# A two-layer attention trunk: shorter scale, gate and combine sequences on VectorE, and one more buffer each for the split q and k and for the split exponentials

## The chip, the core and the metric

The kernel runs on one core of a Trainium2 chip. The metric is the time of one execution on the device, in microseconds (us). The engines of the core are named as in the profile: PE (TensorE, matmuls), PEld (its weight loads), DVE (VectorE), ACT (ScalarE), POOL (GpSimd) and SP (SyncE), whose queue issues every DMA of this kernel. PE, DVE, ACT, POOL and SP each work through their own instructions in the order in which these stand, and wait for one another by semaphores. Lines are written as L345, line 345 of the kernel before.

## The reference, cut to what matters

```python
def reference(x, ...):                       # x: 1 x 1024 x 1024, 16 heads of 64
    for i in range(2):                       # layer 0: FoX, layer 1: dilated windows
        h = rms_norm(x, norm_g[i])
        o, gate = mixer_i(h, ...)
        x = x + (o * jax.nn.silu(gate)) @ w_out
    return x

def fox_mixer(h, ...):                       # causal attention with a forget term
    q, k = rms_norm(q, q_g), rms_norm(k, k_g)
    c = jnp.cumsum(jax.nn.log_sigmoid(f_logit), axis=1)
    s = q @ k * scale + c_q - c_k            # masked, softmax, times v

def dsw_mixer(h, ...):                       # 3 groups: (window, dilation)
    q, k = rotary(rms_norm(q)), rotary(rms_norm(k))
    for g, (window, dilation) in enumerate(((128, 1), (512, 4), (2048, 16))):
        o_g, lse_g = dilated_window_attention(q[g], k[g], v[g], window, dilation)
    wts = jax.nn.softmax(jnp.stack(lses, axis=0), axis=0)
    o = jnp.einsum('gbsh,gbshd->bshd', wts, jnp.stack(outs, axis=0))
```

## The kernel before, in words

**Numbers.** A product of two float32 matrices is made of three float16 products: each side is scaled by a power of two and split into a high and a low half (xh and xl for the rows, the two planes of `w` for the weights), and high times high, high times low and low times high are summed in PSUM (`project`, L340). The scores and the products with v are made in the same way.

**Weights.** They come in blocks of 1024 x 384 (class `Weights`): `load` brings four pieces `raw`, `bound` measures each (DVE L281 the pieces 0 and 2, ACT L279 the pieces 1 and 3, then two small ACT steps L284 and L285), `scale` spreads the measure over the partitions with a small matmul (L252) and works out a power of two in a chain of one-column DVE instructions (L254, L255, L241 to L243, L293, and for a q-k-v block L295, L296, L297 and L300, the last of which keeps a running minimum `low`), and `split` makes the two halves (ACT L310 and DVE L311; one piece of four on POOL, L313 and L315). All of this is done for the next block while the present one is multiplied.

**Stages.** `gates(0)` multiplies out the gate columns of layer 0 and writes silu of them to memory (`gs_d`). Then come 8 pairs of heads of the FoX layer, the output projection of layer 0, `gates(1)`, and 24 blocks of the second layer: 8 pairs of heads of group 0 first, then for each pair of heads the block of group 2 and the block of group 1. The output projection of layer 1 ends it.

**One block of q, k, v.** It has 8 tiles of 128 rows, 24 matmuls each, into one of three PSUM buffers `pj`. Of each tile, DVE multiplies q and k by gains into `u` (L433), ACT squares them (`sq`, L438), and v is split by ACT and DVE (L443, L444); L444 is the last reader of `pj`. For every second tile `heads_pair` normalises two tiles at once: sums (L451, L453), an inverse root by Ln and Exp on ACT (L471 to L473) with a correction on DVE (L474, L475), in layer 1 the rotation on POOL (L465 to L468), the product (L477), and the split of the result into `hl` (ACT L479, POOL L480, DVE L481). A DMA transpose (L485) turns `hl` into `qk_t`, from which PE makes scores (L505). There is one buffer `hl` (`hb=1`).

**Softmax.** Scores are masked and their running extreme is found by one DVE instruction (L745 in the FoX layer, L970 in layer 1), exponentials are taken on ACT (L546, L971), split into `ph` (ACT L549, POOL L552; in layer 1 L975, L976), transposed by DMA into `ptt` (L553, L977) and multiplied with v (L560 to L562). In both layers there are two buffers `ph` and three `ptt`.

**Putting three groups together.** Groups 0 and 2 write unnormalised sums, the row sum and the row extreme to memory (`og_d`, L1083). For each pair of tiles of group 1, `load_cmb` loads the two others and the gate (L1037, L1041), `weigh` finds the common extreme `mm` (DVE L998), makes three weights (POOL L1000, ACT L1001) and weighs and adds groups 0 and 2 on POOL (L1003, L1004), and `combine` on DVE weighs the group's own sums (L1011), adds (L1012), divides (L1014, L1016) and multiplies by the gate (L1019).

**What sets the order.** The order of PE is written out: `Flow` counts slots, four to a tile, and each step of the attention is hung on a slot (`LSD` and `LPD` are the slots from a tile to its scores and from there to the product with v). The order of the other engines is made when the program is built, by a scheduler that goes by priorities and its own estimates.

Of the kernel before, what the change touches and what calls it, by code (L numbers as in the profile page):

```python
# [22 lines left out]
P = 128  # L23
# [29 lines left out]
def tile_cols(g, t):  # L53


    if g < 2:
        return slice(t * P, (t + 1) * P, 1)
    a = 2 * P * (t % 4) + t // 4
    return slice(a, a + 2 * 127 + 1, 2)

# [23 lines left out]
def trunk(ctx, tc, ins, out, cfg):  # L84
# [143 lines left out]
    isx = const.tile([P, 2], F32, name="isx")  # L228
    sy = const.tile([P, 2], F32, name="sy")
    low = const.tile([P, 2], F32, name="low")  # L230
    nc.vector.memset(low, 2.0 ** 60)
# [6 lines left out]
    def root_floor(q):  # L238
# [7 lines left out]
    def spread_sums(src, n, lo, hi):  # L246
# [8 lines left out]
        nc.vector.tensor_scalar(v1, v1, lo, hi, ALU.max, ALU.min)  # L255
        return v1

    under = {}
    turned = set()

    class Weights:
# [10 lines left out]
        def bound(self, i):  # L272
# [4 lines left out]
            if i % 2:  # L277
                jk = sb.tile([P, 2, self.n], F16, name="jk", tag="jk", bufs=1)
                nc.scalar.activation(jk, raw, AF.Square, accum_out=self.vm[:, i : i + 1])  # L279
            else:  # L280
                nc.vector.tensor_reduce(self.vm[:, i : i + 1], raw, AX.XY, ALU.max, apply_absolute_value=True)  # L281
            if i == KT // 2 - 1:
                v = [a.rearrange("p (a b) -> p a b", b=2) for a in (self.vm, self.vm2)]
                nc.scalar.activation(v[1][:, :, 0], v[0][:, :, 0], AF.Square)  # L284
                nc.scalar.copy(v[1][:, :, 1], v[0][:, :, 1])  # L285

        def scale(self):

            e = root_floor(spread_sums(self.vm2, KT // 2, 2.0 ** -40, 2.0 ** 60))
            f = self.f = sm.tile([P, 5], F32, name="ws_f", tag="ws_f")  # L290
            self.sw, t2, self.inv = (f[:, i : i + 1] for i in range(3))
            by, ly = sy if self.kind == "out" else sx, slice(self.layer, self.layer + 1)
            nc.vector.tensor_scalar(self.sw.bitcast(I32), e, -1.0, float(268 << 23), ALU.mult, ALU.add)  # L293
            if self.kind == "qkv":
                nc.vector.tensor_scalar(t2, self.sw, by[:, ly], 2.0, ALU.mult, ALU.max)  # L295
                nc.vector.tensor_scalar(self.sw, t2, 2.0 ** 30, isx[:, ly], ALU.min, ALU.mult)  # L296
                nc.vector.tensor_scalar(t2, t2, 2.0 ** 30, None, ALU.min)  # L297
                self.t2, self.eps = t2, f[:, 3:4]
# [4 lines left out]
            if self.kind != "qkv":  # L303
                nc.vector.reciprocal(self.inv, t2)
# [869 lines left out]
```

## Time and profile before

| | |
|---|---|
| median of 3 runs | 1825.76 us (1823.03 to 1827.61) |
| the profiled execution | 1813.33 us, span 1811.5 us |
| granted PE clock over the span | 0.970 of full speed |
| busy share of the span | PE 92%, DVE 70%, ACT 59%, POOL 48% |
| DMA | 69.8% of 16 engines, 290.44 MB in one queue |

The profile is of one execution; the span runs from its first to its last instruction. A row of a group gives the count, the summed time and the mean of one instruction in ns; behind the bar stands the idle time of the engine just before them, and what ended it. A row of waits gives the total in us, how often, and the longest. A row of the timeline gives start, duration, engine, line and names; the bracket is the idle time before it and its releaser.

### The profile page before, as it was taken

The numbers are of one execution on the slowest core, as the hardware profiler recorded it, in microseconds if no ns is written. First come the engines' busy times: TensorE is split into PE (matmuls) and PEld (weight loads), VectorE is DVE, ScalarE is ACT, GpSimd is POOL, SyncE is SP. The second block draws the span as 40 slices with busy tenths as digits, with TensorE's granted clock in tenths as the row PEclk, the third lists the DMA queues.
The fourth block names the chain that finished last, engine by engine and source line by source line (L and its number), as shares of the span: only waits on it lengthen the run. The fifth ranks groups of instructions, "written<-read, shape, count | busy, mean of one in ns | idle before, by whom it ended". The sixth has DMA issues, their size and how long they took to land.

```text
span 1811.5 us, 38107 instructions
## 1 busy us (share of the span) xinstructions
PE 1659.2 (92%) x13342; PEld 1060.2 (59%) x13342; DVE 1259.9 (70%) x3906; ACT 1068.3 (59%) x2790; POOL 872.5 (48%) x1019
## 2 busy tenths in 40 slices
PE   5899898898888997999999989999899998999999
PEld 3566566566665433756666656656556565565654
DVE  8866677766776557766677786677776777767752
ACT  6555666666666546555666666556555565655630
POOL 4203555555554323125565545556475665646520
PEclk8999999999999998999999999999999999999999
DMA  7334998988889777336777787678676777767742
GB/s 260 122 138 103 191 192 174 168 171 195 191 174 209 205 218 225 109 108 139 141 151 168 149 185 152 138 150 164 153 154 141 157 154 158 161 140 153 190 125 91
DMA packets 658769, 292.88 MB, mean 162 GB/s; under 512 B 510208, under 2 KB 622848, under 8 KB 658576
## 3 DMA queue, kind: packets, MB, share of 16 engines
q1 hardware_dynamic: 658576, 290.44, 69.8%
q8 instruction: 104, 1.70, 0.4%
q14 instruction: 89, 0.73, 0.1%
HBM read 124.35 MB, written 41.22 MB: 91 GB/s over the span
## 4 chain that ended last, share of the span: by engine, by line
PE 36%; DVE 12%; DMA 11%; POOL 5%; issue 5%; ACT 3%; SPq 0%; DVEq 0%; POOLq 0%; ACTq 0%
PE pj L345 24%; PE pj L369 8%; DMA qk_t<-hl 6%; PE s L505 2%; DMA raw<-in_w_dsw 2%; DVE p L970 2%; DVE w L311 2%; DVE hl L481 1%; POOL hl L480 1%; POOL ph L976 1%; DVE pj L451 1%; POOL cmb L1003 1%; DMA ptt<-ph 1%; DVE vm L281 1%; POOL raw L313 1%
## 5 line engine op out<-in xcount | busy, mean ns | idle before, releaser
L345 PE MATMUL pj<-w,xh 128*128 128x384 f16 (+2 forms) x4864 | 1191.2, 329 | 32.7 <-DVE vt L444 18.3
L345 PE MATMUL pj<-w,xl 128*128 128x384 f16 (+2 forms) x2432 | 799.1, 329 | 4.8 <-DVE xl L898 2.6
L345 PEld LDWEIGHTS <-xh 128*128 128x128 f16 x4864 | 473.8, 99 | 322.5 <-issue 48.1
L345 PEld LDWEIGHTS <-xl 128*128 128x128 f16 x2432 | 241.4, 99 | 166.7 <-issue 10.6
L552 POOL TENSOR_TENSOR ph<-p,ph 128x512 f16<-128x512 f32 (+3 forms) x176 | 179.1, 1036 | 190.8 <-ACT ph L549 181.3
L480 POOL TENSOR_TENSOR hl<-u,hl 128x512 f16<-128x512 f32 x128 | 153.9, 1203 | 131.5 <-ACT hl L479 131.3
L976 POOL TENSOR_TENSOR ph<-p,ph 128x768 f16<-128x768 f32 (+2 forms) x96 | 154.0, 1604 | 119.4 <-ACT ph L975 116.1
L505 PE MATMUL s<-qk_t 128*128 128x128 f16 (+1 forms) x1504 | 162.9, 249 | 51.2 <-DMA qk_t<-hl 40.1
L311 DVE SCALAR_TENSOR_TENSOR w<-raw,ws_f,w 128x768 f16<-128x768 f32 (+2 forms) x133 | 181.5, 1379 | 9.6 <-ACT w L310 9.5
L369 PE MATMUL pj<-xh,w 128*128 128x512 f16 x512 | 162.0, 386 | 0.0
L505 PEld LDWEIGHTS <-qk_t 128*128 128x128 f16 x1504 | 113.6, 99 | 70.8 <-DMA qk_t<-hl 44.4
L479 ACT CAST hl<-u 128x512 f16<-128x512 f32 x128 | 78.8, 616 | 120.0 <-DMA qk_t<-hl 90.0
L444 DVE SCALAR_TENSOR_TENSOR vt<-pj,vt 128x128 f16<-128x128 f32 x256 | 73.3, 289 | 109.1 <-ACT vt L443 107.1
L438 ACT ACTIVATE sq<-pj 128x256 f32<-128x256 f32 x256 | 96.2, 376 | 76.7 <-DVE u L433 68.0
L546 ACT ACTIVATE p<-p,acc 128x512 f32<-128x512 f32 (+2 forms) x192 | 108.1, 608 | 36.0 <-DVE acc L745 33.2
L560 PEld LDWEIGHTS <-ptt 128*128 128x128 f16 x1136 | 106.9, 99 | 38.1 <-DMA ptt<-ph 26.0
L369 PEld LDWEIGHTS <-w 128*128 128x128 f16 x768 | 75.2, 100 | 86.2 <-issue 7.0
L549 ACT CAST ph<-p 128x512 f16<-128x512 f32 (+3 forms) x176 | 87.7, 537 | 64.2 <-DMA ptt<-ph 63.8
L310 ACT ACTIVATE w<-raw,ws_f 128x768 f16<-128x768 f32 (+2 forms) x133 | 116.9, 911 | 13.7 <-DVE ws_f L293 13.7
L279 ACT ACTIVATE jk<-raw 128x768 f16<-128x768 f32 (+2 forms) x88 | 72.3, 821 | 85.5 <-DMA raw<-in_w_dsw 43.6
L465 POOL TENSOR_TENSOR ra<-u,cs 128x128 f32<-128x128 f32 x96 | 50.3, 524 | 148.7 <-DVE u L433 69.8
L433 DVE TENSOR_TENSOR u<-pj,gr 128x256 f32<-128x256 f32 x256 | 106.2, 415 | 17.2 <-PE pj L345 16.9
(212 smaller groups left out, 2916.5 us busy)
## 6 DMA issues: line engine op xcount, KB each, us to landing
raw<-in_w_dsw SPq DMA_DIRECT2D x96, 384.0 KB, 3.9
raw<-in_w_fox SPq DMA_DIRECT2D x32, 384.0 KB, 4.2
og_d<-og SPq DMA_DIRECT2D x64, 132.0 KB, 2.8
cmb<-og_d SPq DMA_DIRECT2D x64, 132.0 KB, 2.8
bc<-c_d SPq DMA_DIRECT2D x32, 256.0 KB, 4.6
gs_d<-ge SPq DMA_DIRECT2D x32, 192.0 KB, 2.1
xt<-in_xt SPq DMA_DIRECT2D x16, 256.0 KB, 3.8
gsf<-gs_d SPq DMA_DIRECT2D x64, 64.0 KB, 2.5
```

What stands on the lines that cost most here:

```text
L310: nc.scalar.activation(w[:, 0, :, :n], raw, AF.Copy, scale=self.sw)
L311: nc.vector.scalar_tensor_tensor(w[:, 1, :, :n], raw, self.sw, w[:, 0, :, :n], ALU.mult, ALU.subtract)
L345: nc.tensor.matmul(ps[:, :n], a[:, k, cols], w.slab(k, j), start=(k == 0 and i == 0), stop=(k == KT - 1 and i == 2))
L369: nc.tensor.matmul(ps[m], w.slab(k, j)[:, m * P : (m + 1) * P], a[:, k, 512 * b : 512 * (b + 1)], start=(k == 0 and x == 0), stop=(k == KT ...
L433: nc.vector.tensor_mul(u[:, t % 2].rearrange("p (a b) d -> p a b d", a=2), ps[:, : 4 * HD].rearrange("p (a b d) -> p a b d", a=2, b=2), gr ...
L438: nc.scalar.activation(sq[:, t % 2], ps[:, : 4 * HD], AF.Square)
L480: nc.gpsimd.tensor_sub(hl[:, :, :4, 1], u, hl[:, :, :4, 0])
L505: nc.tensor.matmul(s[:, c0 : c0 + cnt * P].rearrange("p (c s) -> p c s", c=cnt), qk[:, i, blk], kk[:, j : j + cnt, e], start=(h == 0), sto ...
L546: nc.scalar.activation(p, p, AF.Exp, bias=acc, scale=-1.0)
L552: (nc.gpsimd if pool_l else nc.vector).tensor_sub(ph[:, e, 1, cols], p, ph[:, e, 0, cols])
L560: nc.tensor.matmul(o[:, e, :], hi, vt[:, j, e, HD:], start=(b == 0), stop=False, skip_group_check=True)
L976: nc.gpsimd.tensor_sub(ph[:, 1], st["p"], ph[:, 0])
```

## The change

It has these parts.

- **Scales.** The clamp L255 goes; `root_scale` makes in three instructions what L241 to L243 and L293 made in four. For q-k-v blocks two clamps and a product become one clamp against limits that are worked out once per layer (`lim`, L295 to L297 become one), and each scale is kept in its own column of `sws`, so that the running minimum L300 is one reduction at the end. On ACT the two steps L284 and L285 become one.
- **Gates.** L536 (product) and L537 (largest value) become one DVE instruction that also leaves the largest value, on 48 tiles.
- **Inverse root.** The Ln on ACT (L471) reads the sums in PSUM with `eps` as its bias and no longer waits for L453, which stays for the correction.
- **Combine with a joint maximum.** `mm` is found ahead of the exponentials of group 1, which then use it as their bias. So the group's own weight is one: L1011 goes, the weights are two instead of three. The reciprocal is multiplied into the gate on POOL instead of into the sums on DVE (L1016), but for the last pair of heads, where DVE does it. `load_cmb` is hung 9 slots earlier (7 before the scores instead of 2 behind), and allocates `cmb`.
- **Order of group 2.** Its 8 tiles are taken as 0, 4, 1, 5, 2, 6, 3, 7 (`nth_tile`), so that a pair of tiles holds what one pair of group 1 needs.
- **Buffers.** `hl` 1 to 2; in the FoX layer `ptt` 3 to 4 and `ph` 2 to 3; in layer 1 `cmb` 3 to 4, `ph` 2 to 3, and the loaded gate gets four buffers of its own (`gsd`).

```diff
-    def root_floor(q):
+    def root_scale(dst, q, k):
         e = q.bitcast(I32)
         nc.vector.tensor_scalar(e, e, 1, 0x7FC00000, ALU.logical_shift_right, ALU.bitwise_and)
-        nc.vector.tensor_scalar(e, e, float(127 << 22), None, ALU.add)
-        nc.vector.tensor_single_scalar(e, e, 0x7F800000, ALU.bitwise_and)
-        return e
+        nc.vector.tensor_scalar(e, e, -1.0, float((k << 23) - (127 << 22)), ALU.mult, ALU.add)
+        nc.vector.tensor_single_scalar(dst.bitcast(I32), e, 0x7F800000, ALU.bitwise_and)
...
         nc.vector.tensor_reduce(v1, ws, AX.X, ALU.add)
-        nc.vector.tensor_scalar(v1, v1, lo, hi, ALU.max, ALU.min)
...
-                nc.vector.tensor_scalar(t2, self.sw, by[:, ly], 2.0, ALU.mult, ALU.max)
-                nc.vector.tensor_scalar(self.sw, t2, 2.0 ** 30, isx[:, ly], ALU.min, ALU.mult)
-                nc.vector.tensor_scalar(t2, t2, 2.0 ** 30, None, ALU.min)
-                nc.scalar.activation(self.eps, t2, AF.Square, scale=EPS ** 0.5)
-                nc.vector.tensor_tensor(low[:, ly], low[:, ly], self.sw, ALU.min)
+                self.sw, self.eps, m = sws[:, self.layer, n : n + 1], f[:, 2:3], lim[:, self.layer]
+                nc.vector.tensor_scalar(self.sw, f[:, 0:1], m[:, 0:1], m[:, 1:2], ALU.max, ALU.min)
+                nc.scalar.activation(self.eps, self.sw, AF.Square, scale=m[:, 2:3])
...
-        nc.scalar.activation(r, v, AF.Ln)
+        nc.scalar.activation(r, w["ss"], AF.Ln, scale=1.0 / HD, bias=w["eps"])
...
-                nc.vector.scalar_tensor_tensor(e, e, w.inv, ps, ALU.mult, ALU.mult)
-                nc.vector.tensor_reduce(peak[:, layer, h * NT + t : h * NT + t + 1], e, AX.X, ALU.max, apply_absolute_value=True)
+                nc.vector.tensor_tensor_reduce(e, e, ps, w.inv, 0.5, ALU.mult, ALU.max, peak[:, layer, h * NT + t : h * NT + t + 1])
...
-                    nc.scalar.activation(p[:, e], p[:, e], AF.Exp, bias=acc[:, e : e + 1], scale=-1.0)
+                    if joint is None:
+                        nc.scalar.activation(p[:, e], p[:, e], AF.Exp, bias=acc[:, e : e + 1], scale=-1.0)
+            if joint is not None:
+                mm = joint().rearrange("p (i e) -> p i e", e=2)
+                for i in range(2):
+                    p = st["p"][:, at[i] : at[i + 1]].rearrange("p (e k) -> p e k", e=2)
+                    for e in range(2):
+                        nc.scalar.activation(p[:, e], p[:, e], AF.Exp, bias=mm[:, i, e : e + 1], scale=-1.0)
...
-        nc.vector.tensor_mul(o, o, cmb[2][:, 0].unsqueeze(2).broadcast_to([P, N2, HD + 1]))
         nc.vector.tensor_add(o, o, cmb[0][:, 1, :, :, : HD + 1].rearrange("p t e d -> p (t e) d"))
         den = sm.tile([P, N2], F32, name="den", tag="den")
         nc.vector.reciprocal(den, o[:, :, HD])
-        y = o[:, :, :HD]
-        nc.vector.tensor_mul(y, y, den.unsqueeze(2).broadcast_to([P, N2, HD]))
+        (nc.vector if hp == NHP - 1 else nc.gpsimd).tensor_mul(gv, gv, den.unsqueeze(2).broadcast_to([P, N2, HD]))
...
-        nc.vector.tensor_mul(y2, y, gv)
+        nc.vector.tensor_mul(y2, o[:, :, :HD], gv)
...
+            ps = project(w, tile_cols(g, nth_tile(g, t)))
...
-                dsw_pair(g, t0, qks, vt, done, get, LSD, LPD)
-                flow.at(flow.now + LSD + 2, lambda hp=hp, t0=t0, cmb=cmb: load_cmb(hp, t0, cmb))
+                flow.at(flow.now + LSD - cfg["lcm"], lambda hp=hp, t0=t0, cmb=cmb: load_cmb(hp, t0, cmb))
+                dsw_pair(g, t0, qks, vt, done, get, LSD, LPD, lambda cmb=cmb: joint_most(cmb))
```

The order of PE is the same in both programs, row by row; the other engines' orders differ. Three places show how. In all of them the lines of the changed kernel are its own: its L440 is L433 of before, L451 is L444, L445 is L438.

DVE in layer 1, where the scale of the next block is worked out beside the end of a combine; before, from the product with the gate to the running minimum (`ws_f` holds the scale, `low` the minimum, `y` the combined rows):

```order
L1019 TENSOR_TENSOR y_17903<-ob,gsd 128x256
L242 TENSOR_SCALAR v_17852<-v_17852 128x1
L453 TENSOR_SCALAR rs_v<-pj,ws_f 128x8
L243 TENSOR_SCALAR v_17852<-v_17852 128x1
L293 TENSOR_SCALAR ws_f<-v_17852 128x1
L295 TENSOR_SCALAR ws_f<-ws_f,sx 128x1
L444 SCALAR_TENSOR_TENSOR vt<-pj,vt 128x2x64
L433 TENSOR_TENSOR u<-pj,gr 128x256
L296 TENSOR_SCALAR ws_f<-ws_f,isx 128x1
L474 SCALAR_TENSOR_TENSOR pj<-pj,rs_v 128x8
L297 TENSOR_SCALAR ws_f<-ws_f 128x1
L300 TENSOR_TENSOR low<-low,ws_f 128x1
```

The same place in the changed kernel, to the first split of the next weights:

```order
L458 TENSOR_REDUCE pj<-sq 128x8
L247 TENSOR_SCALAR ws_f<-v_17660 128x1
L461 TENSOR_SCALAR rs_v<-pj,ws_f 128x8
L299 TENSOR_SCALAR sws<-ws_f,lim 128x1
L1035 TENSOR_TENSOR y_17709<-ob,gsd 128x256
L451 SCALAR_TENSOR_TENSOR vt<-pj,vt 128x2x64
L440 TENSOR_TENSOR u<-pj,gr 128x256
L312 SCALAR_TENSOR_TENSOR w<-raw,sws,w 128x768
```

The scale ends after one clamp (`sws`), and the split of the weights follows the next tile's L451 and L440 at once.

ACT in a block of group 1, two pairs of tiles; before, the exponentials have the group's own extreme (in `cmb`) as bias, and `wt` is the weights' exponential:

```order
L438 ACTIVATE sq<-pj 128x256
L971 ACTIVATE p<-p,cmb 128x128 x2
L971 ACTIVATE p<-p,cmb 128x256 x2
L471 ACTIVATE rs_y<-rs_v 128x8
L443 ACTIVATE vt<-pj 128x2x64
L1001 ACTIVATE wt<-wt 128x12
L975 CAST ph<-p 128x768
```

In the changed kernel the bias is `mm`, and `wt` has 8 columns:

```order
L450 ACTIVATE vt<-pj 128x2x64
L985 ACTIVATE p<-p,mm 128x128 x2
L985 ACTIVATE p<-p,mm 128x256 x2
L1019 ACTIVATE wt<-wt 128x8
L479 ACTIVATE rs_y<-pj,ws_f 128x8
L989 CAST ph<-p 128x768
L480 ACTIVATE rs_y<-rs_y 128x8
```

All four exponentials stand behind `mm`, and the next tile's instructions behind them as before.

POOL in the changed kernel at the end of a combine in group 1; the new row is the product of gate and reciprocal (`gsd<-gsd,den`), the split of a weight piece is `raw<-raw,sws`:

```order
L473 TENSOR_TENSOR ra<-u,cs 128x128
L474 TENSOR_TENSOR rb<-u,sn 128x8x8
L475 TENSOR_TENSOR rb<-u,sn 128x8x8
L1032 TENSOR_TENSOR gsd<-gsd,den 128x256
L1018 TENSOR_TENSOR wt<-mm,cmb 128x8
L476 TENSOR_TENSOR u<-ra,rb 128x8x16
L314 TENSOR_SCALAR raw<-raw,sws 128x768
L990 TENSOR_TENSOR ph<-p,ph 128x768
```

The new product stands between the rotation's rows and ahead of the weights' split and of the split of the exponentials; before, no such row stood on POOL.

More of the change, by code (lines that the diff above doesn't have):

```diff
@@ L59, in tile_cols, with nth_tile @@
     return slice(a, a + 2 * 127 + 1, 2)
+def nth_tile(g, t):
+    return t // 2 + 4 * (t % 2) if g == 2 else t
 class Flow:
@@ L276, in bound @@
             raw = self.raw[i][:, :, : self.n]
-            if i % 2:
+            if i not in cfg["most"]:
                 jk = sb.tile([P, 2, self.n], F16, name="jk", tag="jk", bufs=1)
-                nc.scalar.activation(jk, raw, AF.Square, accum_out=self.vm[:, i : i + 1])
+                with nc.allow_low_precision(reason="a bound within a factor of two is enough"):
+                    nc.scalar.activation(jk, raw, AF.Square, accum_out=self.vm2[:, i : i + 1])
             else:
                 nc.vector.tensor_reduce(self.vm[:, i : i + 1], raw, AX.XY, ALU.max, apply_absolute_value=True)
[L282 to L285, printed above, removed]
+            if i == max(cfg["most"]):
+                c = slice(0, i + 1, 2)
+                nc.scalar.activation(self.vm2[:, c], self.vm[:, c], AF.Square)
@@ L827, in trunk @@
         kts = []
[L828 removed]
+        vt = v_tile(w)
         for t in range(NT):
```

79 lines of the change are left out of this document (44 added, 35 removed).

## The prediction

> **What bounds the kernel now.** I read the page's head first, then the busy time stage by stage, then PE's waits in the two long stages, then the waits of the engine that PE waits for.
>
> ```profile
> span 1811.5 us, 38107 instructions
> PE 1659.2 (92%) x13342; PEld 1060.2 (59%) x13342; DVE 1259.9 (70%) x3906; ACT 1068.3 (59%) x2790; POOL 872.5 (48%) x1019
> core 0: us, PE busy (x) PEld busy (x) DVE busy (x) ACT busy (x) POOL busy (x), PEclk, DMA share, GB/s
> 0.00:109.00 109.00, 81.12 (x520) 55.52 (x521) 89.54 (x230) 64.97 (x151) 34.07 (x36) 0.92 0.50 168
> 180.00:514.00 334.00, 297.45 (x3062) 206.37 (x3061) 231.91 (x769) 216.04 (x543) 181.01 (x171) 0.96 0.87 180
> 514.00:690.00 176.00, 150.63 (x1135) 85.83 (x1132) 110.72 (x281) 105.78 (x206) 73.29 (x63) 0.93 0.82 213
> 764.00:1022.00 258.00, 254.05 (x2077) 164.87 (x2076) 179.71 (x562) 160.98 (x435) 129.89 (x160) 1.00 0.67 142
> 1022.00:1646.00 624.00, 586.83 (x4687) 376.44 (x4686) 460.38 (x1566) 375.25 (x1110) 369.15 (x497) 0.98 0.73 155
> ```
>
> PE is the bound, and the change takes no matmul from it. So all that can be won is PE's idle time and the slower clock. The rows are stages: start with gates, FoX pairs (180 to 514), their tail with the output projection, group 0 (764 to 1022), groups 2 and 1 (1022 to 1646). Group 0 has nothing left (258 - 254.05 = 3.95 us idle). FoX has 334 - 297.45 = 36.6 us idle, groups 2 and 1 have 624 - 586.83 = 37.2. Who ends it, FoX first, then groups 2 and 1:
>
> ```profile
> PE o L560 <- DMA ptt<-ph: 19.5, 13, 3.4
> PE s L505 <- DMA qk_t<-hl: 10.0, 5, 2.2
> PE s L505 <- DVE acc L745: 6.9, 9, 1.6
> ACT ph L549 <- DMA ptt<-ph: 58.3, 29, 5.4
> ...
> PE s L505 <- DMA qk_t<-hl: 21.0, 16, 4.7
> PE pj L345 <- DVE vt L444: 15.2, 7, 2.9
> ACT hl L479 <- DMA qk_t<-hl: 68.3, 23, 4.5
> DVE mm L998 <- DMA cmb<-og_d: 16.1, 7, 3.2
> SPq L1037 <- DMA og_d<-og: 27.1, 14, 3.8
> ```
>
> The three PE rows of FoX make 36.4 of 36.6 us, the two of groups 2 and 1 make 36.2 of 37.2. The reason behind them differs. In FoX ACT stands 58.3 us for a free `ph` and does not appear for `hl`; in groups 2 and 1 it stands 68.3 us for the one `hl`. Whatever follows in ACT's queue (squares, v halves, exponentials) stands too.
>
> **FoX: the third `ph`, the fourth `ptt`.** One stall from the timeline, SP, then ACT, PE, DVE:
>
> ```profile
> 321.83 4.70 SPq L553 DMA_TRANSPOSE ptt<-ph  x1
> 329.14 0.41 ACT L549 CAST ph<-p 128x256 f16<-128x256 f32 x1 [5.39 <-DMA ptt<-ph]
> 329.09 0.20 PE L560 MATMUL o<-vt,ptt 128*128 128x65 f16 x1 [2.89 <-DMA ptt<-ph]
> 329.87 0.69 DVE L451 TENSOR_REDUCE pj<-sq 128x8 f32<-128x512 f32 x1 [3.75 <-ACT sq L438]
> ```
>
> One transpose, whose issue alone held SP 4.70 us, lands at 329.1. ACT has stood 5.39 us for it, DVE's L451 3.75 us behind ACT. A third `ph` takes away these two waits. It does not take away PE's own 2.89 us here, since PE needs that very transpose. So I take a quarter of the `ptt` wait (19.5 / 4 = 4.9: transposes that start earlier since their ACT work did), a quarter of the `qk_t` wait (2.5; its transpose is behind the same SP queue), and two thirds of the wait for DVE (6.9 x 2/3 = 4.6, scores that wait for a PSUM buffer which DVE, late behind ACT, hasn't read). Sum 12.0, a third of the idle time. Ends: 0, if DMA at a share of 0.87 gives the time back as later landings, and 36.6.
>
> **Groups 2 and 1: the second `hl`, and DVE's queue.** The waits for `qk_t` come in a loop: cast into `hl`, transpose, landing, cast of the next. A second buffer cuts it, and what is late next is the DVE work ahead of the cast; I take two thirds, 21.0 x 2/3 = 14.0. The wait for L444 is DVE's backlog where the block of group 1 ends and the split of the next weights falls beside two combines. DVE and PE there:
>
> ```profile
> 1273.07 0.48 DVE L444 SCALAR_TENSOR_TENSOR vt<-pj,vt 128x128 f16<-128x128 f32 x2
> 1273.41 0.48 PE L345 MATMUL pj<-w,xh 128*128 128x384 f16 x2 [1.92 <-DVE vt L444]
> ```
>
> What DVE loses, by groups of the whole run:
>
> ```profile
> L300 DVE TENSOR_TENSOR low<-low,ws_f 128x1 f32<-128x1 f32 x32 | 24.1, 754 | 0.0
> L1011 DVE TENSOR_TENSOR ob<-ob,wt 128x260 f32<-128x260 f32 x32 | 13.7, 428 | 4.9 <-PE ob L562 4.5
> L1016 DVE TENSOR_TENSOR ob<-ob,den 128x256 f32<-128x256 f32 x32 | 13.6, 425 | 0.3
> L255 DVE TENSOR_SCALAR v<-v 128x1 f32<-128x1 f32 x46 | 6.7, 145 | 0.2
> L293 DVE TENSOR_SCALAR ws_f<-v 128x1 int32<-128x1 int32 x44 | 6.6, 150 | 0.6
> L295 DVE TENSOR_SCALAR ws_f<-ws_f,sx 128x1 f32<-128x1 f32 x32 | 6.6, 207 | 0.3
> L297 DVE TENSOR_SCALAR ws_f<-ws_f 128x1 f32<-128x1 f32 x32 | 4.9, 153 | 0.8
> L537 DVE TENSOR_REDUCE peak<-ge 128x1 f32<-128x384 f32 (+1 forms) x48 | 24.0, 501 | 0.8
> ```
>
> A pair of heads has two scales and four combines: 2 x (754 + 145 + 150 + 207 + 153) = 2.8 us and 4 x (428 + 425) = 3.4 us, 6.2 in all. About half falls in the crowded stretch (one scale 1.4, two combines 1.7), 3.1 us, against waits of 15.2 / 7 = 2.2. That covers the wait where all else stays; I take four fifths, 12.2, since DVE also stands there for other things. Sum 26.2, or 26.2 / 37.2 = 0.7 of the idle time. The ends are 0 and 37.2.
>
> **The clock.** After a wait PE runs slower for a while:
>
> ```profile
> 1196.98 0.48 PE L345 MATMUL pj<-w,xh 128*128 128x384 f16 x2 [2.51 <-DVE vt L444]
> 1198.76 0.85 PE L345 MATMUL pj<-w,xh 128*128 128x384 f16 x2
> 1201.58 0.49 PE L345 MATMUL pj<-w,xh 128*128 128x384 f16 x2
> ```
>
> Two matmuls took 0.85 instead of 0.49 us from soon behind a wait of 2.51 us. The granted clock is 0.96 in FoX (334 x 0.04 = 13.4 us lost) and 0.98 in groups 2 and 1 (12.5 us). I count half of that as lost within waits that are counted already; of the other half goes what goes of the waits: 6.7 x 1/3 = 2.2 and 6.2 x 0.7 = 4.4. Ends 0 and 12.9. The Trainium skill ("TensorE: Matmul & The Clock Gate", Part 1: The HAM clock gate) has the clock fall only after an idle window of about 3.4 us. By that rule a wait of 2.51 us would cost nothing more, and the forecast would be 6.6 us later; the rows show that it does, and the sum goes by them.
>
> **Gates, scales elsewhere, tail.** L537 falls away on 48 tiles, but its DVE time is beside matmuls: group 0, with the same weight scales and tiles, has PE idle for 4 us of 258, so I cost these and the ACT edits (L284/L285, Ln without L453) at 0; without that cover it would be at most L537's 24.0 us. From 514 to 690 the same buffers serve the last pair of FoX: of 176 - 150.63 = 25.4 us idle I take 2 (ends 0 and 8). The start (109 - 81.12 = 27.9 us idle) stays.
>
> **What is added.** POOL gets 28 products of gate and reciprocal. The nearest rows:
>
> ```profile
> L1004 POOL TENSOR_TENSOR cmb<-cmb 128x260 f32<-128x260 f32 x32 | 28.7, 896 | 1.3
> L481 DVE COPY hl<-hl x128: 261/294/1525, 150.5 to 1724.7; 128x512 f16<-128x512 f16 x128
> 1263.92 2.36 POOL L315 TENSOR_TENSOR w<-raw,w 128x768 f16<-128x768 f32 x1
> 1264.90 1.52 DVE L481 COPY hl<-hl 128x512 f16<-128x512 f16 x1
> ```
>
> At 896 ns that is 28 x 0.9 = 25 us of POOL, which was busy 369.15 of 624. DVE's last product now stands behind it, with 2 or more other DVE rows between it and the reciprocal in the program, and SP's write of `y` behind that. The copy L481, 294 ns in the median, took 1.52 us while POOL worked at L315, and ended with it. L300's 754 ns for one column may be the same. So a POOL row can hold DVE: between 0 and 28 x 0.9 = 25 us of DVE time, below zero excluded since only work is added. The joint maximum lets four exponentials wait for `mm`, and `mm` for the loads of `cmb`, which it already awaited for 16.1 us. The loads go out 9 slots earlier, and group 2's new order takes away what SP stood for (27.1 us at L1037); the exponentials then have 7 slots of cover. I take 3 us of PE time for all of this (range 0 to 25).
>
> **Sum.** 12.0 + 26.2 + 2.2 + 4.4 + 2 - 3 = 43.8, say 44 us. The profiled execution goes from 1813.33 to 1769; the runs' median lies 12.4 us above that execution, so from 1825.76 to 1782. A measurement of this kernel can tell about 0.3%, or 5 us, from no change.
>
> **Rivals.**
>
> 1. *All waits go* (12%). With buffers and a lighter DVE, nearly all idle time of both stages and the clock behind it go: 36.6 + 37.2 + 12.9 = 87, with 8 from the FoX tail 95, so 1731. For: the PE rows account for all idle time. Against: the 2.89 us above, whose cause stays.
> 2. *Small gain: DMA in FoX, POOL's hold on DVE* (18%). FoX gives nothing, as DMA at 0.87 sets its pace, and of the second stage's 26.2 + 4.4 the POOL rows take back 25 us times DVE's busy share there (460.38 / 624 = 0.74), 18.5: 12 us stay, 1814. For: the 4.70 us issue, the 1.52 us copy. Against: the new POOL rows add 25 us to 873. The Trainium skill ("SBUF — State Buffer", Who interferes with whom) says that a DVE copy in a two-port mode and a POOL instruction exclude each other for a whole instruction; the 1.52 us agrees.
> 3. *The change doesn't reach PE* (6%): another wait takes each removed one's place, within 5 us of 1825.76.
> 4. *Slower: the joint maximum holds ACT and DVE* (9%). In each of 32 pairs `mm` waits for `cmb`, and behind it in DVE's queue stands L444, which frees `pj`. If each waits the 2.3 us of today's seven (16.1 / 7) and all reach PE, 74 us are lost against 44: 1856. It decides from 44 / 32 = 1.4 us a pair. Against: loads 9 slots earlier, and today 25 of 32 wait for nothing.
>
> **Chances.** The forecast, a gain of 25 to 75 us, has 55%. With rivals 1 and 2 that is 85% faster by over 0.3%, 6% within, 9% slower. The range leaves out rivals 3 and 4: from rival 1, 1731, to just past rival 2, 1815.
>
> **What would show it.** Right: ACT's waits at the casts into `ph` in FoX and into `hl` in groups 2 and 1 gone, PE's wait for L444 at the end of group 1 nearly gone, L505's wait for `qk_t` down by two thirds there and by a quarter in FoX, granted clock at 0.99 in groups 2 and 1, PE idle about 11 us there and 25 in FoX. Wrong: PE waiting for DVE's last product or `mm`, DVE waiting for `cmb` in most pairs, or FoX's idle time unchanged while its DMA share rises.

## The result and the profile after

The changed kernel took 1908.22 us in the median (1908.0 to 1908.71, 4 runs) against 1826.23 (1823.03 to 1827.61, 4 runs): a ratio of 1.0452, 95% interval 1.0434 to 1.047. It is slower by 82 us; the forecast was 44 us faster, with 1815 as the upper end of its range. The profiled execution after spans 1906.1 us, 94.6 more than before.

The head of the page of after: VectorE has 239 rows and 55 us less work, as intended, and TensorE (PE), with as many matmuls as before, is busy longer.

```profile
span 1906.1 us, 37858 instructions
PE 1679.0 (88%) x13342; PEld 1067.7 (56%) x13342; DVE 1204.8 (63%) x3667; ACT 1079.8 (57%) x2746; POOL 885.9 (46%) x1047
```

To place the loss I cut both traces at the matmul that sums each weight block's bound (L252 before, L255 after), which PE passes once a block. First before, then after: six FoX blocks, seven blocks of group 0, sixteen of groups 2 and 1. As in the prediction, a row gives the stretch and its length, the busy time of PE, PEld, DVE, ACT and POOL, the granted PE clock, the DMA share and GB/s. (The prediction's "group 0", 764 to 1022, was cut early: group 2 begins at about 1096. Its last stretch held two blocks of group 0.)

```profile
173.00:504.00 331.00, 295.31 (x3032) 204.57 (x3031) 229.53 (x765) 213.39 (x538) 179.20 (x169) 0.96 0.87 181
828.00:1104.00 276.00, 264.87 (x2285) 174.07 (x2284) 201.81 (x625) 181.95 (x492) 155.12 (x182) 0.99 0.76 157
1104.00:1727.00 623.00, 587.90 (x4630) 376.34 (x4627) 457.38 (x1590) 371.01 (x1107) 368.44 (x507) 0.98 0.72 155
```

```profile
171.00:501.00 330.00, 297.57 (x3034) 205.90 (x3033) 221.82 (x738) 219.34 (x536) 171.06 (x170) 0.96 0.89 182
828.00:1149.00 321.00, 278.06 (x2285) 178.04 (x2284) 208.39 (x588) 187.50 (x485) 153.66 (x182) 0.95 0.66 136
1149.00:1822.00 673.00, 598.60 (x4633) 379.54 (x4630) 422.73 (x1457) 371.24 (x1092) 392.43 (x535) 0.96 0.66 143
```

FoX is level, and both kernels reach 828 together. Group 0, costed at nothing, loses 45 us and groups 2 and 1 lose 50; the rest of the span is level. PE's idle time is 321 - 278.06 = 42.9 us in group 0 and 74.4 us in groups 2 and 1 (11.1 and 35.1 before), and the clock fell from 0.99 and 0.98 to 0.95 and 0.96.

The waits of before in the same blocks of group 0, then of groups 2 and 1:

```profile
ACT sq L438 <- DVE u L433: 15.2, 18, 1.5
PE s L505 <- DMA qk_t<-hl: 10.3, 9, 4.7
...
PE pj L345 <- DVE vt L444: 17.0, 7, 2.9
PE s L505 <- DMA qk_t<-hl: 14.3, 14, 3.4
PE pj L345 <- DVE u L477: 0.9, 2, 0.5
```

The waits of after: FoX, then group 0, then groups 2 and 1.

```profile
PE o L567 <- DMA ptt<-ph: 11.5, 10, 2.1
ACT ph L556 <- DMA ptt<-ph: 10.9, 6, 2.5
PE s L513 <- DMA qk_t<-hl: 10.4, 6, 2.0
PE s L513 <- DVE acc L752: 4.7, 4, 1.4
...
ACT sq L445 <- DVE u L440: 61.9, 32, 4.4
PE s L513 <- DMA qk_t<-hl: 32.4, 8, 5.0
DVE vm L285 <- DMA raw<-in_w_dsw: 9.8, 8, 2.4
...
ACT jk L283 <- DMA raw<-in_w_dsw: 46.2, 19, 4.8
PE s L513 <- DMA qk_t<-hl: 37.9, 16, 5.0
PE pj L346 <- DVE u L485: 28.0, 7, 4.3
PE pj L346 <- DVE vt L451: 7.2, 8, 0.9
```

ScalarE's (ACT) wait for a free `ph` in FoX fell to 10.9 us, and the one for the one `hl` is gone, as forecast. But PE does not have the time: it waits longer for `qk_t`, and 28.0 us in place of 0.9 for `u`, the normalised q and k. In group 0 ACT stands 61.9 us for VectorE's (DVE) gain product (15.2 before), and DVE stands there for raw weights, which it did not before.

One block of group 0 on the timeline of after: DVE, SyncE (SP), ACT and PE; the figure in brackets is the idle time ahead.

```profile
921.79 2.45 DVE L312 SCALAR_TENSOR_TENSOR w<-raw,sws,w 128x768 f16<-128x768 f32 x1
924.36 3.12 DVE L312 SCALAR_TENSOR_TENSOR w<-raw,sws,w 128x768 f16<-128x768 f32 x2
929.52 0.95 DVE L285 TENSOR_REDUCE vm<-raw 128x1 f32<-128x768 f32 x1 [1.83 <-DMA raw<-in_w_dsw]
930.39 0.41 DVE L440 TENSOR_TENSOR u<-pj,gr 128x256 f32<-128x256 f32 x1
...
924.27 0.35 SPq L273 DMA_DIRECT2D raw<-in_w_dsw  x1
924.70 4.32 SPq L991 DMA_TRANSPOSE ptt<-ph  x1
...
930.84 0.38 ACT L445 ACTIVATE sq<-pj 128x256 f32<-128x256 f32 x1 [4.38 <-DVE u L440]
...
933.58 0.50 PE L346 MATMUL pj<-w,xh 128*128 128x384 f16 x2 [1.77 <-DVE u L485]
942.11 1.25 PE L513 MATMUL s<-qk_t 128*128 128x128 f16 x7 [3.73 <-DMA qk_t<-hl]
```

DVE makes three weight splits (L312) in a row. The first ends at 924.24 and frees a raw buffer; SP issues the load into that buffer at 924.27; and a few rows on DVE stands for that load, at the bound L285. Behind it wait the gain product of a finished tile, then ACT's square (4.38 us idle), then `u`, its transpose and PE. The program says why. DVE's rows there, before and after, from the first split to the bound (the rows left out are eight ISA rows, two to each score product):

```
L311 SCALAR_TENSOR_TENSOR w_11426<-raw_11039,ws_f_11380,w_11426 128x768
L474 SCALAR_TENSOR_TENSOR pj_11298<-pj_11298,rs_v_11390 128x8
L444 SCALAR_TENSOR_TENSOR vt_11255<-pj_11413,vt_11255 128x2x64
L475 SCALAR_TENSOR_TENSOR pj_11298<-pj_11298,rs_y_11400 128x8
L477 TENSOR_TENSOR u_11292<-u_11292,pj_11298 128x512
L311 SCALAR_TENSOR_TENSOR w_11532<-raw_11053,ws_f_11380,w_11532 128x768
L433 TENSOR_TENSOR u_11445<-pj_11451,gr_109 128x256
L311 SCALAR_TENSOR_TENSOR w_11611<-raw_11074,ws_f_11380,w_11611 128x768
...
L281 TENSOR_REDUCE vm_12442<-raw_12163 128x1
```

```
L312 SCALAR_TENSOR_TENSOR w_11290<-raw_10909,sws_118,w_11290 128x768
L451 SCALAR_TENSOR_TENSOR vt_11125<-pj_11167,vt_11125 128x2x64
L312 SCALAR_TENSOR_TENSOR w_11396<-raw_10923,sws_118,w_11396 128x768
L312 SCALAR_TENSOR_TENSOR w_11475<-raw_10944,sws_118,w_11475 128x768
L451 SCALAR_TENSOR_TENSOR vt_11125<-pj_11277,vt_11125 128x2x64
L285 TENSOR_REDUCE vm_12300<-raw_12021 128x1
L440 TENSOR_TENSOR u_11309<-pj_11315,gr_109 128x256
```

Before, the bound stood 9 rows behind the last split, with eight score rows (four products) between; now it stands 2 rows behind. It waits for the buffer that the first split frees: from that one it is 16 rows before and 5 now.

### The profile page after: what moved, and what is told of

Same layout as the page of the kernel before. It is cut to its first block, busy times and chain, and to the rows that moved or that the text cites. A ratio compares the mean times of both kernels' runs of the same rounds, so it can differ in the third digit from the quotient of the medians.

```text
span 1906.1 us, 37858 instructions
## 1 busy us (share of the span) xinstructions
PE 1679.0 (88%) x13342; PEld 1067.7 (56%) x13342; DVE 1204.8 (63%) x3667; ACT 1079.8 (57%) x2746; POOL 885.9 (46%) x1047
## 4 chain that ended last, share of the span: by engine, by line
PE 39%; DMA 12%; DVE 10%; issue 6%; ACT 5%; POOL 5%; SPq 1%; DVEq 0%; POOLq 0%; ACTq 0%
PE pj L346 27%; PE pj L370 6%; DMA qk_t<-hl 6%; PE s L513 3%; DMA raw<-in_w_dsw 3%; DVE w L312 3%; POOL hl L488 1%; POOL w L316 1%; DVE hl L489 1%; ACT w L311 1%; DVE u L440 1%; DVE p L977 1%; DVE xs L901 1%; DMA raw<-in_w_gate 1%; POOL cmb L1021 1%
## 5 line engine op out<-in xcount | busy, mean ns | idle before, releaser
L559 POOL TENSOR_TENSOR ph<-p,ph 128x512 f16<-128x512 f32 (+3 forms) x176 | 171.1, 992 | 190.3 <-ACT ph L556 96.0
L513 PE MATMUL s<-qk_t 128*128 128x128 f16 (+1 forms) x1504 | 167.9, 255 | 98.8 <-DMA qk_t<-hl 91.6
L488 POOL TENSOR_TENSOR hl<-u,hl 128x512 f16<-128x512 f32 x128 | 148.6, 1161 | 161.8 <-ACT hl L487 161.1
L445 ACT ACTIVATE sq<-pj 128x256 f32<-128x256 f32 x256 | 96.5, 377 | 184.2 <-DVE u L440 150.6
L990 POOL TENSOR_TENSOR ph<-p,ph 128x768 f16<-128x768 f32 (+2 forms) x96 | 160.3, 1670 | 79.2 <-ACT ph L989 77.1
L440 DVE TENSOR_TENSOR u<-pj,gr 128x256 f32<-128x256 f32 x256 | 107.0, 418 | 111.5 <-PE pj L346 111.5
L312 DVE SCALAR_TENSOR_TENSOR w<-raw,sws,w 128x768 f16<-128x768 f32 x96 | 139.6, 1468 | 18.8 <-ACT w L311 18.2
L979 ACT ACTIVATE p<-p,og 128x128 f32<-128x128 f32 (+1 forms) x256 | 96.8, 438 | 46.9 <-DVE og L977 46.5
L285 DVE TENSOR_REDUCE vm<-raw 128x1 f32<-128x768 f32 (+2 forms) x88 | 81.4, 925 | 66.2 <-DMA raw<-in_w_dsw 32.7
L451 DVE SCALAR_TENSOR_TENSOR vt<-pj,vt 128x128 f16<-128x128 f32 x256 | 74.1, 289 | 73.8 <-ACT vt L450 73.0
```

The source lines that it names most:

```text
L312: nc.vector.scalar_tensor_tensor(w[:, 1, :, :n], raw, self.sw, w[:, 0, :, :n], ALU.mult, ALU.subtract)
L440: nc.vector.tensor_mul(u[:, t % 2].rearrange("p (a b) d -> p a b d", a=2), ps[:, : 4 * HD].rearrange("p (a b d) -> p a b d", a=2, b=2), gr ...
L445: nc.scalar.activation(sq[:, t % 2], ps[:, : 4 * HD], AF.Square)
L488: nc.gpsimd.tensor_sub(hl[:, :, :4, 1], u, hl[:, :, :4, 0])
L513: nc.tensor.matmul(s[:, c0 : c0 + cnt * P].rearrange("p (c s) -> p c s", c=cnt), qk[:, i, blk], kk[:, j : j + cnt, e], start=(h == 0), sto ...
L559: (nc.gpsimd if pool_l else nc.vector).tensor_sub(ph[:, e, 1, cols], p, ph[:, e, 0, cols])
```

## The experiments

**Theory A**: the shorter scale chain lets the scheduler place the splits in a row and the bound on the next raw weights right behind them; A1 puts the price on standing there for the data, A2 on the splits. **Rivals**: B, Ln on TensorE's bank; C, the new combination (its parts are numbered run by run; in the first four texts C is instead that the added buffers let transposes pile up); D, the buffers only pass waits on; E, something in the new chain itself or moved addresses; F, the second `hl` makes the FoX gain. The table has what was measured: the median, the ratio to the kernel before with its interval, and from the profiled execution the mean block of FoX, the mean block of group 0, and the mean pair of blocks of groups 2 and 1 (us, six of each between those matmuls). The kernel before, run beside each set, had medians of 1822 to 1827 us.

| kernel | median | ratio | FoX | gr. 0 | pair |
|---|---|---|---|---|---|
| before | 1826.23 | 1 | 55.2 | 38.0 | 77.0 |
| after | 1908.22 | 1.0452 (1.0434-1.047) | 54.9 | 45.1 | 83.3 |
| after_old_scale | 1843.4 | 1.0105 (1.0074-1.0136) | 53.5 | 38.4 | 80.7 |
| before_new_scale | 1899.0 | 1.0396 (1.0365-1.0428) | 55.6 | 45.5 | 78.3 |
| after_more_raw | 1859.62 | 1.0177 (1.014-1.0214) | 55.0 | 40.2 | 83.1 |
| after_old_ln | 1907.39 | 1.0468 (1.0423-1.0512) | 52.7 | 45.7 | 83.6 |
| after_padded_chain | 1881.48 | 1.0309 (1.0271-1.0346) | 54.9 | 38.4 | 87.3 |
| before_buffers | 1792.86 | 0.9825 (0.9787-0.9862) | 50.9 | 38.0 | 78.0 |
| before_fox_buffers | 1805.66 | 0.9901 (0.9871-0.9931) | 51.9 | 37.9 | 77.8 |
| before_hl_buffer | 1819.12 | 0.9968 (0.9942-0.9994) | 55.2 | 38.1 | 77.3 |
| before_joint | 1841.3 | 1.0101 (1.0068-1.0135) | 56.6 | 38.0 | 77.6 |
| before_joint_shift | 1831.16 | 1.0044 (1.0024-1.0064) | 55.7 | 38.0 | 77.6 |
| after_old_scale_comb | 1804.08 | 0.9893 (0.9844-0.9941) | 52.5 | 38.2 | 76.3 |
| after_old_scale_raw | 1844.77 | 1.0108 (1.0072-1.0144) | 53.7 | 38.0 | 80.9 |
| old_scale_gate_on_vector | 1839.35 | 1.0074 (1.0049-1.01) | 53.5 | 38.1 | 81.2 |
| after_no_bounds | 1830.33 | 1.0029 (1.0002-1.0056) | 53.9 | 39.0 | 78.4 |
| buffers_no_bounds | 1764.57 | 0.9661 (0.9614-0.9709) | 53.8 | 37.7 | 71.5 |
| no_bounds_old_comb | 1817.65 | 0.9954 (0.9935-0.9972) | 53.6 | 39.0 | 76.9 |
| no_bounds_no_joint | 1793.51 | 0.9822 (0.9786-0.9858) | 54.4 | 38.9 | 74.0 |
| buffers_more_raw | 1779.6 | 0.9743 (0.9715-0.977) | 51.2 | 37.5 | 75.2 |

**The scale chain, taken back and alone.** The chain's lines, as in the change:

```
-            e = root_floor(spread_sums(self.vm2, KT // 2, 2.0 ** -40, 2.0 ** 60))
...
-                nc.vector.tensor_scalar(t2, self.sw, by[:, ly], 2.0, ALU.mult, ALU.max)
-                nc.vector.tensor_scalar(self.sw, t2, 2.0 ** 30, isx[:, ly], ALU.min, ALU.mult)
+            root_scale(f[:, 0:1], spread_sums(self.vm2, KT // 2), 268)
...
+                nc.vector.tensor_scalar(self.sw, f[:, 0:1], m[:, 0:1], m[:, 1:2], ALU.max, ALU.min)
```

> The changed kernel with the scale chain of the kernel before (its L288-L304, the row scale and the two constants made from it, the running minimum); buffers, Ln, gates, bounds and the combination stay changed. Theory A (the shorter chain brings VectorE's three weight splits forward into one row and the bound of the next block, whose buffer those splits release, right behind them): the eight group-0 blocks go back from about 45 us to 38-39 us, the sum to 1810-1860 us. Rival B (Ln now reads TensorE's accumulator bank and ties ScalarE to it) and rival C (the added buffers let more transposes pile up): nothing comes back, 1895-1915 us.

> The kernel before with the new scale chain alone. Theory A: it holds the loss alone; group-0 blocks go from 38 to about 45 us, the sum to 1870-1920 us. Rivals B and C: 1815-1835 us, no change or a little less.

Both as theory A has it: without it the changed kernel gains 65 us, and alone it costs 74 us, with group 0 at 38.4 and 45.5. Pairs get back only 83.3 to 80.7. Of what the chain alone costs, the profiled execution has 48 us in the seven blocks of group 0; some 16 lie ahead of layer 1 and some 15 in groups 2 and 1, whose cause was not followed up.

**Two passes that nothing needs.**

```
+                for _ in range(2):
+                    nc.vector.tensor_scalar(f[:, 0:1], f[:, 0:1], 1.0, None, ALU.mult)
                 nc.vector.tensor_scalar(self.sw, f[:, 0:1], m[:, 0:1], m[:, 1:2], ALU.max, ALU.min)
```

> The changed kernel with two VectorE passes more in each qkv scale chain (a 128x1 column times 1.0, twice: nothing needs them), which makes the chain five dependent passes long after the sum again and puts nine rows in place of two between the last weight split and the bound of the next block. Theory A (it is the order that the shorter chain brings, not an instruction in it): more work gives less time: group-0 blocks 38-39 us in place of 45, sum 1840-1870 us. Rival E (something in the new chain itself, such as reading the scale from a column of a shared tile, or the moved addresses): blocks stay at 44-46 us, sum 1905-1915 us.

More work, less time: blocks of 38.4 us and 27 us off the sum. Every buffer has the address that it has in the changed kernel and the new chain is there, so E is ruled out for group 0; the order there is the old one again, with 16 rows between the split that frees the buffer and the bound. The sum missed my range, since pairs went the other way, to 87.3: PE's wait for `u` goes from 28.0 to 40.7 us. In the pairs the passes did not move the bounds away: the same distance, one for each block of a pair, is 4 and 6 rows there, 5 and 3 in the changed kernel, 7 and 14 in the kernel before, and 7 and 11 with the old chain. This fits theory A, but was not varied by itself in the pairs.

**The wait or the splits.** First more raw buffers, then no later bounds (`like` is the first qkv block of layer 1):

```
-rbufs=8
+rbufs=11
```

```
         def bound(self, i):
+            if self.like is not None:
+                return
...
-            root_scale(f[:, 0:1], spread_sums(self.vm2, KT // 2), 268)
+            root_scale(f[:, 0:1], spread_sums((self.like or self).vm2, KT // 2), 268)
```

> The changed kernel with eleven buffers of raw weights in place of eight, so that three of the four loads of a block wait no longer for the splits of the block ahead; the three splits still stand in one row on VectorE. Theory A in its first form (A1: VectorE stands before the next block's raw data): VectorE's wait for raw data in group 0 (12.1 us) goes below 3 us, blocks to 38-40 us, sum 1810-1865 us. In its second form (A2: the splits in one row hold the gain products and sums of the tiles behind them): blocks stay at 43-45 us, sum 1890-1910 us. Rivals B and C: 1895-1915 us.

> The changed kernel, but layer 1's 23 later qkv blocks take the first block's sums for their scale: their four bounds each (two reductions of VectorE, two squares of ScalarE) are left out, and with them every wait of these engines for raw weights; the splits still stand in one row. Theory A1 (the wait before raw data is the price): group-0 blocks 38-39 us and pairs 77-78 us, sum 1795-1825 us. Theory A2 (the splits in one row): group-0 blocks 42 us or more. Theory C (the combination itself holds the pairs): group-0 blocks 38-39 us, pairs 80 us or more, sum 1825-1850 us.

The waits in group 0 of the first (same blocks as in the fence of after):

```profile
ACT sq L445 <- DVE u L440: 21.4, 18, 2.7
DVE vm L285 <- DMA raw<-in_w_dsw: 9.4, 9, 2.4
PE s L513 <- DMA qk_t<-hl: 8.3, 8, 2.8
```

With more buffers the bound stands 16 rows behind the splits, which stay in a row and are as long as in after (median 2193 ns in both; 1572 before). ACT's wait falls from 61.9 to 21.4 us and the block to 40.2, yet DVE still waits 9.4 us for raw weights, where I had expected under 3. So what costs is not how long DVE stands there, as A1 had it, but what stands behind it. Without the bounds the block is 39.0 (pairs and sum, 78.4 and 1830.33, lie just outside A1's ranges). The splits in a row, A2, are left with 1 to 2 us a block, the place of the bound with 5 to 6.

**Ln.**

```
-        nc.scalar.activation(r, w["ss"], AF.Ln, scale=1.0 / HD, bias=w["eps"])
+        nc.scalar.activation(r, v, AF.Ln)
```

> The changed kernel, but Ln reads the sum with eps from SBUF again, as before the change (rs_v, not TensorE's bank). Rival B: ScalarE's waits for rs_v and for the gain product fall, group-0 blocks 38-40 us, sum 1810-1865 us. Theory A and rival C: 1895-1915 us.

No change in the sum or in group 0: B falls.

**The buffers, alone.** On the kernel before all of these lines, then the second pair, then the first:

```
-hb=1
+hb=2
-l1=dict(ga=7, ptt=3, ph=2
+l1=dict(ga=7, ptt=4, ph=3
-l2=dict(ga=4, cmb=3, ptt=3, ph=2
+l2=dict(ga=4, cmb=3, ptt=3, ph=3
```

> The kernel before with the added buffers alone (hl 2, FoX ph 3 and ptt 4, layer-1 ph 3). The forecast's terms for them (FoX 12, second hl 14, their clock about 5, tail 2) give 1790-1797 us. Theory D (a buffer only passes the wait on: what ScalarE waited for hl turns into TensorE's and ScalarE's waits for the next qk_t and products) gives FoX blocks of 52-53 us in place of 55.5, pairs of group 2 and 1 unchanged at 77 us, sum 1808-1826 us.

> The kernel before with the third ph and the fourth ptt in the FoX layer alone. The forecast's term is 12 us with a clock term beside it: 1808-1814 us. Theory D (these two are what shortened FoX by 25 us with all buffers together): FoX blocks 50-52 us, sum 1795-1805 us. Rival F (the second hl did it, so that the products no longer wait for the turn of q and k): FoX blocks 54-55.5 us, sum 1815-1826 us.

> The kernel before with the second hl alone. The forecast's term is 14 us and two thirds of the wait for qk_t in the pairs: 1806-1812 us, pairs 75 us. Theory D (ScalarE's wait for hl is cover, and only moves): pairs 77-78 us, sum 1820-1830 us. Rival F: FoX blocks 51-53 us, sum 1800-1812 us.

Together they gain 29 us. That is near the 28 of the forecast's buffer terms (12.0, 14.0 and 2), but by luck, since the terms are not where the gain is. FoX, then groups 2 and 1 of the kernel with all buffers (stretches first, waits then):

```profile
170.00:476.00 306.00, 285.11 (x3037) 202.01 (x3036) 224.52 (x767) 215.45 (x542) 173.99 (x170) 0.99 0.94 197
1083.00:1708.00 625.00, 585.45 (x4627) 375.26 (x4624) 457.91 (x1590) 371.81 (x1108) 368.45 (x508) 0.99 0.72 155
```

```profile
ACT hl L479 <- DVE u L477: 52.8, 32, 4.2
PE s L505 <- DMA qk_t<-hl: 22.1, 14, 3.6
PE pj L345 <- DVE vt L444: 12.8, 7, 2.5
```

FoX gains 25 us: 14.8 of PE's idle time and 10.2 of its busy time, with the clock at 0.99. DMA carried it at a share of 0.94, so 0.87 was not its limit. Groups 2 and 1 gain nothing: ACT's wait for the turn has become a wait for `u`, and PE still waits for `qk_t`. By themselves the FoX pair gains 18 us and the second `hl` 5, with FoX blocks of 51.9 and 55.2: F falls, and D holds but for those 5 us, which is less than the differences that the last section leaves open.

**The combination.** Alone (its hunks of the change); alone with the layer's buffers back at their old address; taken out together with the scale chain; then, on the changed kernel with the old scale chain, with raw weights loaded earlier, and with one product back on VectorE. The edits of the second, fourth and fifth:

```
-        wt = sm.tile([P, 2, N2], F32, name="wt", tag="wt")
+        wt = sm.tile([P, 3, N2], F32, name="wt", tag="wt")[:, :2]
```

```
-rbufs=8
+rbufs=11
-wload=(18, 20, 22, 24)
+wload=(10, 12, 14, 18)
```

```
-        (nc.vector if hp == NHP - 1 else nc.gpsimd).tensor_mul(gv, gv, den.unsqueeze(2).broadcast_to([P, N2, HD]))
+        nc.vector.tensor_mul(gv, gv, den.unsqueeze(2).broadcast_to([P, N2, HD]))
```

> The kernel before with the new combination alone (joint maximum ahead of group 1's exponentials, gate times reciprocal on GpSimd, group 2's tiles in the new order, earlier cmb loads). Theory C (the combination lengthens the stretch in which group 1's last tiles and group 2's first meet): pairs from 77.1 to 80-82 us, sum 1845-1860 us. The forecast (added work 3 us, passes saved off the path): 1815-1830 us.

> The new combination alone, as before, with the weights' tile kept at three columns of four (two are used), so that the layer's buffers start at the address of the kernel before and not 128 bytes lower; the order of every engine is that of the new combination alone. If the 20 us that the combination lost ahead of its own first instruction come from the address: layer 1 begins within 5 us of the kernel before (828 us), sum 1822-1830 us. If not: 1838-1847 us.

> The changed kernel with both the scale chain and the combination of before: buffers, Ln, gates and bounds remain. Theories A and C together: group-0 blocks 38 us, pairs 76-77 us, FoX blocks 52 us, sum 1805-1825 us. If the combination costs nothing: as with the old scale alone, 1838-1850 us. By the forecast's buffer terms: 1785-1797 us.

> The changed kernel with the scale chain of before, eleven raw buffers and loads of raw weights eight slots earlier (six for the last), the combination kept. Theory A carried on (what is left in pairs of group 2 and 1 is ScalarE standing before raw data, 40.5 us there, in an order that puts the squares ahead of their data): ScalarE's wait for raw in these pairs below 15 us, pairs 77 us or less, sum 1805-1825 us. Theory C (the combination itself holds): pairs stay at 80 us or more, sum 1835-1850 us.

> The changed kernel with the scale chain of before and the product of gate and reciprocal on VectorE for all heads again (GpSimd loses 28 products of 612 ns). Theory C1 (the product on GpSimd makes the combination late and SyncE's queue with it): pairs from 80.5 to 77-78 us, sum 1815-1828 us. Theory C2 (joint maximum or earlier loads): pairs 80-82 us, sum 1838-1850 us.

Alone it leaves the pairs at 77.6. It lost 1.0% (0.4% at the old address, just outside that text's range), and in the profiled execution 20 of its 28 us lie ahead of the first row in which any engine's order differs from before; the last section comes back to that. With buffers, Ln and gates beside it, it costs 4.4 us a pair and 39 us in all (1843.4 against 1804.08). The fourth run settles nothing: ACT's wait for raw weights in the pairs stayed at 40.7 us. The product on GpSimd (POOL), C1 of the last text, is not the price: pairs stay at 81.2, and the sum moves by 4 us, which the two intervals don't tell from nothing.

One place of the pairs in after, where group 1 ends: ACT, DVE, PE.

```profile
1410.61 0.84 ACT L283 ACTIVATE jk<-raw 128x768 f16<-128x768 f32 x1 [1.93 <-DMA raw<-in_w_dsw]
1414.43 0.84 ACT L283 ACTIVATE jk<-raw 128x768 f16<-128x768 f32 x1 [2.89 <-DMA raw<-in_w_dsw]
...
1412.97 0.95 DVE L285 TENSOR_REDUCE vm<-raw 128x1 f32<-128x768 f32 x1 [1.00 <-DMA raw<-in_w_dsw]
1413.85 0.16 DVE L1011 TENSOR_REDUCE mm<-cmb 128x4 f32<-128x12 f32 x1
1414.06 0.41 DVE L1035 TENSOR_TENSOR y<-ob,gsd 128x256 f32<-128x256 f32 x1
1414.39 0.68 DVE L485 TENSOR_TENSOR u<-u,pj 128x512 f32<-128x512 f32 x1
...
1415.12 0.80 PE L346 MATMUL pj<-w,xh 128*128 128x384 f16 x2 [4.04 <-DVE u L485]
```

Both engines stand before raw weights again; DVE has the joint maximum and the combination's product ahead of `u`, and PE idles 4.04 us, once in each of the seven pairs seen (28.0 us).

**The pairs without bounds.** With the raw weights out of the way, the buffers as a control, then the combination or its joint maximum taken back. The edit of the last:

```
-                dsw_pair(g, t0, qks, vt, done, get, LSD, LPD, lambda cmb=cmb: joint_most(cmb))
+                dsw_pair(g, t0, qks, vt, done, get, LSD, LPD)
...
+        nc.vector.tensor_mul(o, o, cmb[2][:, 0].unsqueeze(2).broadcast_to([P, N2, HD + 1]))
```

> The control: the kernel before with the added buffers, and the same later bounds left out. By theory A1 these bounds stood behind their data in this order, so that only their work goes (1.9 us a block on each of two engines that are not the bound): group-0 blocks 37.7-38 us, pairs 76-78 us, sum 1780-1793 us. If bounds cost the pairs much in every order, pairs go to 73-75 us and the sum below 1775 us.

> The changed kernel without layer 1's later bounds (their scale comes from the first block's sums) and with the combination of before; buffers, scale chain, Ln and gates stay changed. Theory C (the combination costs the pairs 6 us once nothing else is late): pairs 72-74 us, sum 1780-1795 us. If scale chain, Ln or gates hold the pairs: 77-79 us, sum 1820-1832 us.

> The changed kernel without the later bounds and with the exponentials of group 1 at their own maximum, the three weights and the product of sums and weight on VectorE as before; order of group 2's tiles, earlier loads and GpSimd's product of gate and reciprocal stay changed. Theory C1 (the joint maximum, for which all four products and then four exponentials of a pair must wait): pairs 72-75 us, sum 1785-1805 us. Theory C2 (the rest of the combination): pairs 77-79 us, sum 1820-1835 us.

The control surprised me: without the bounds pairs need 71.5 us (78.0 with them), so they cost pairs 6.5 us in the old order too. Taking the joint maximum back, with the third weight and DVE's product that go with it, gains 37 us and 4.4 a pair. Fifteen blocks of groups 2 and 1 and PE's waits in them, with the joint maximum, then without:

```profile
1140.00:1740.00 600.00, 550.85 (x4313) 351.78 (x4312) 384.07 (x1349) 324.65 (x963) 375.51 (x509) 0.98 0.67 151
```

```profile
PE s L521 <- DMA qk_t<-hl: 25.0, 15, 2.9
PE pj L354 <- DVE vt L459: 17.3, 7, 2.7
PE pj L354 <- DVE u L493: 5.3, 1, 5.3
```

```profile
1143.00:1708.00 565.00, 539.83 (x4311) 348.31 (x4309) 391.55 (x1378) 338.99 (x965) 376.77 (x510) 1.00 0.75 161
```

```profile
PE s L521 <- DMA qk_t<-hl: 22.0, 15, 3.1
PE pj L354 <- DVE vt L459: 0.9, 1, 0.9
```

One wait of PE in each pair is gone, for v's second half (L459), which frees `pj`: over these rows 47.6 us become 22.9, and PE's busy time falls by 11.0 at the full clock. My expectation for the whole combination missed (76.9 for 72-74): the rest of the new combination is better than the old, and its joint maximum worse.

**The fastest that computes the whole.** The kernels without bounds leave out 23 measurements of weights that the computation asks for; this one leaves out nothing.

> The kernel before with the added buffers and eleven raw buffers. If the waits for raw weights still cost time where the order is the old one (22.5 us of ScalarE in the pairs): sum 1775-1787 us. If they are cover there: 1788-1798 us.

With `rbufs=11` beside the buffers the computation takes 1779.6 us, 2.6% less than before.

## Why the prediction was wrong

- **The step that failed** is "group 0, with the same weight scales and tiles, has PE idle for 4 us of 258, so I cost these ... at 0; without that cover it would be at most L537's 24.0 us". I costed a removed pass as work that goes, and took the rest of the queue as fixed. But the scheduler lays the queue out anew; five passes fewer moved a bound in front of a gain product, and that cost 45 us in group 0 (the edit alone: 48 there, 74 in all). The rows of DVE's order were there to be read. No rival had this.
- **"Two thirds, 21.0 x 2/3 = 14.0" for the second `hl`** failed: alone it gained 5 us (0.9968), and pairs stayed at 77.3. The 21.0 us held two blocks of group 0 with 7.6 of them; the sixteen blocks of groups 2 and 1 have 14.3. ACT's 68.3 us was the cover of a longer chain; when it went, ACT waited for `u`.
- **"Four fifths, 12.2" for the passes** failed: PE's wait for L444 became 7.2 us, but 28.0 us for `u` stand in its place.
- **FoX** was right in its mechanism and mis-sized: 12.0 us of idle time and 2.2 of clock were forecast; with the buffers alone 14.8 of idle time and 10.2 of PE's busy time went, so the clock term was the one mis-sized. Rival 2's limit by DMA was wrong (a share of 0.94 was reached). The 2 us for the tail did not come: with all buffers the tail from 476 to 769 is 293 us, against 287. In the changed kernel FoX stays at 330 us; which edits took the gain back there is not settled (its blocks take 54.9 us, 52.7 with the old Ln, 53.5 with the old chain; 50.9 with the buffers alone; one execution each).
- **"I take 3 us ... (range 0 to 25)" for what is added** was too small: the joint maximum cost 37 us where the bounds were out. Rival 4 had this mechanism and its sign, but its way is not what the rows show: DVE's wait for `cmb`, 18.7 us before, is gone in after. Nor was it the main loss of group 0. POOL's 28 products, 25 us of its time in the forecast, were worth 4 us at most that the runs can tell (1843.4 against 1839.35).
- **The clock** did not go to 0.99 but down to 0.95 and 0.96, in the two stages where PE's idle time grew; it was costed as part of waits that would shrink, and they grew. One such wait costs more than its length: behind the 2.51 us that the prediction shows, the granted clock was 0.50 for 3.40 us (1198.10 to 1201.50), which is 1.7 us of PE's work.

Open: why pairs stay at 74.0 without bounds and joint maximum against the control's 71.5; which of buffers, Ln and gates makes the combination cost 4.4 us a pair, where alone it costs 0.6; and whether the place of the bounds is what the padded chain costs the pairs.

## What to carry to other kernels

Where a scheduler orders the queues, read the new order around each shortened chain before costing it: look for an instruction that now stands right behind the one that frees its input's buffer, and for what stands behind it. Here a wait of ACT or DVE, which feed PE, was worth its time only where what came next in the queue was ready; test a buffer alone before adding its wait to a sum.

## What the runs showed that was not expected

- The same order is not the same time. The new combination alone has every engine's rows through FoX as in the kernel before, yet its FoX blocks took 56.6 us for 55.2, and 55.7 with the buffers back at their address. And the buffers kernel without bounds has FoX's rows in the order of the buffers kernel, with what follows the constants moved by 32 bytes. FoX took 323 us for 306. The landings of its transposes, the buffers kernel first (us in the last column):

```profile
ptt<-ph SPq DMA_TRANSPOSE x73, 3.8
...
qk_t<-hl SPq DMA_TRANSPOSE x25, 4.0
```

```profile
ptt<-ph SPq DMA_TRANSPOSE x73, 4.2
...
qk_t<-hl SPq DMA_TRANSPOSE x25, 4.7
```

  Whether the addresses do this was not separated from the spread of executions; differences of some 10 us between kernels here should not be read as the edit's.
- In group 0 the 21 weight splits on DVE took 2193 ns in the median, and 1572 before. In the block shown above the first two ran beside POOL's part of the split and took 2.45 and 2.19 us, the third, with POOL idle, 1.00.
